# RWKV units of a decoder layer: v, the scaled key and the scaled keys turned by block-exchanging transfers and VectorE instead of TensorE

## The chip, the cores and the metric

One core of one Trainium2 chip runs one launch of the kernel. The metric is the device time of that launch in microseconds (us). The kernel before was run three times: 1602.31, 1606.76 and 1600.2 us, median 1602.31. A further execution ran under the profiler; its own time was 1607.54 us, and its trace spans 1605.8 us.

## The reference

The program is one layer of a decoder for a prompt of 1024 tokens and eight sample requests of eight tokens, at width 1024, in fp32:

```python
h = rms_norm(x, norm_mix) * (1 + sc) + sh
P = h @ w_in                      # 1792 RWKV columns, 512 pool columns, 2 x 1024 gates
o_r = rwkv7_branch(...)           # 8 heads of 64: r, decay, k, v, kk, a
o_p = pool_branch(...)
merged = sigmoid(g_r) * (o_r @ w_br_rwkv) + sigmoid(g_p) * (o_p @ w_br_pool)
x = x + gt * (merged @ w_out)
x = x + gt * (square(relu(h2 @ w_ff1)) @ w_ff2)
# in the RWKV branch, token by token:
sa = einsum("bhvk,bhk->bhv", S, -kk_t)
S = S * w_t + sa (x) (kk_t * a_t) + v_t (x) k_t
y = einsum("bhvk,bhk->bhv", S, r_t)
```

The outputs are the layer's result after a last norm and the new states. The recurrence over tokens is what the changed functions belong to.

## The kernel before

Every activation is kept with its features on the 128 partitions and its 1088 tokens (1024 and 64) in the free dimension, in tiles called `wt`, `hx`, `px` and so on. A large product is cut into output blocks of 128 features ("jobs"); each is computed in fp32 as three matmuls (weights high by input high, high by low, low by high) over three token pieces of 364, 362 and 362 columns, so TensorE sees runs of 128x362 matmuls such as `mm<-hx,whi` and `mm<-hx,wlo`. The weights of a half job arrive in `wraw` (256 KB on SyncE's queue), ScalarE rounds them to `whi`, VectorE subtracts to `wlo`.

**Phase 1** overlaps two streams on TensorE. The back stream is jobs: all of `w_in` (its inputs are the sixteen `hx` tiles of the normed x), then eight jobs of the pool half of the branch merge ("op jobs", whose inputs `hx<-d_oph`, `hx<-d_opl` are read back from DRAM into the same sixteen buffers). The fore stream is the RWKV branch, two heads at a time, f = 0 to 3: `scores` (three units: prompt chunks 0 to 7, the sample tokens, prompt chunks 8 to 15; a chunk is 64 tokens), then `main` (the inverse of each chunk's triangle, `level`, `affine`) beside `fill` (the bonus and, for f over 0, `post(f-1)`: the group norm and gate), with a sequential chain of state steps `S` per chunk running along. After the last head pair comes `post(3)`, whose two `hx` tiles (here called orr[3], high and low) are the last inputs of the RWKV half of the branch merge ("or jobs"), the first work of **phase 2**. Each or job takes its inputs in quarters, and orr[3] is the fourth quarter.

TensorE's order is written out by a planner (`Pace`) that prices every instruction with an estimate and puts fore work between job matmuls when its inputs should be ready; TensorE then executes exactly that order, and waits where an estimate was too low. The `need(...)` calls tell the planner what a fore step waits for. The other engines' orders are set by a scheduler at build time; each engine and each issuing queue executes its own order strictly.

A prompt unit (`unit`, u = 0 or 1) starts with `ra` (r and the scaled key, 128 x 8 x 2 x 64), multiplies it with `bk` (key and b) to the masked scores `ab`, `at`, `ak` (matmuls `w<-ra,bk`), scales `bk` by the chunk's end decay, and then turns three things so that tokens, not features, lie on partitions: v (16 matmuls of 64x64 with an identity, `w<-kct,wt`), the scaled key (16, `w<-kct,ra`) and the scaled `bk` (8 transposes of 128x128, `w<-kct,bk`). ScalarE copies v into `uv` and the turned `bk` into `ab`; VectorE copies the scaled key into `at`. The product `w<-uv,at` is the first reader of the turned v (scaled key and `bk` are first read in `level` and `affine`). `K.mm` is line 358, the transposes `K.tr` line 389, and every instruction of another engine is recorded at line 187.

SyncE issues nearly all transfers of this phase (`wraw`, the spills `d_x<-d`, `d_th<-px`, the reads `wt<-d_x`, `hx<-d_oph`). An fp32 matmul is recorded twice, so the counts of the profile are twice those of the program.

Of the kernel before, what the change touches and what calls it, by code (L numbers as in the profile page):

```python
# [12 lines left out]
AF = mybir.ActivationFunctionType  # L13
# [7 lines left out]
NPR = 1024  # L21
NSEQ = 8
TS = 8
NT = NPR + NSEQ * TS
# [202 lines left out]
class Room:  # L227


    wait = 0  # L230
# [91 lines left out]
class K:  # L322
# [592 lines left out]
    def unit(self, f, d, u):  # L915
# [14 lines left out]
        if prompt:  # L930
            at = Q["at"] = tl("at", [2, 64])
            ak = at[:, :, 1, :]
            strict, incl = self.kc("strict"), self.kc("incl")
        else:
            strict, incl = self.kc("strict8"), self.kc("incl8")
            ak = Q["ak"] = tl("ak", [64])
        for a in range(0, C, 4):
            m = min(4, C - a)
            us = slice(a, a + m)
            cu = slice(c0 + a, c0 + a + m)  # L940
            yield self.need(bk[:, cu], ra[:, us], banks=("w", "w"))
            pss = [self.ps("w") for _ in HB]
            for i in range(m):
                for hs, ps in zip(HB, pss):
                    self.mm(ps[:, i * 128:(i + 1) * 128], bk[hs, c0 + a + i, :, :].rearrange("p s j -> p (s j)"),
                            ra[hs, a + i, :, :].rearrange("p s j -> p (s j)"), start=True, stop=True)
            for h, (hs, ps) in enumerate(zip(HB, pss)):
                os = HB[1 - h]
                pv = ps[:, :m * 128].rearrange("p (c s j) -> p c s j", s=2, j=64)
                nc.vector.tensor_tensor(ab[:, us, h, 0:64], pv[:, :, 0, :], incl.unsqueeze(1).to_broadcast([P, m, 64]), op=ALU.mult)  # L950
                nc.vector.tensor_tensor(ak[hs, us, :], pv[hs, :, 1, :], strict[hs].unsqueeze(1).to_broadcast([64, m, 64]), op=ALU.mult)
                for b in range(2):
                    rq = slice(os.start + 32 * b, os.start + 32 * b + 32)
                    src = pv[rq, :, 1, 32 * b:32 * b + 32]
                    if prompt:
                        nc.scalar.activation(ad[rq, cu, :], src, AF.Copy)
                        if b == 0:
                            nc.scalar.activation(ao[rq, cu, :], pv[rq, :, 1, 32:64], AF.Copy)
                    else:
                        nc.vector.tensor_tensor(ad[rq, 16, :], src[:, 0, :], strict[rq, 32 * b:32 * b + 32], op=ALU.mult)  # L960
        bh = bk[:, cs, :, :].rearrange("p c s j -> p c (s j)")
        if prompt:
            nc.vector.tensor_tensor(bh, bh, end[:, cs].unsqueeze(2).to_broadcast([P, C, 128]), op=ALU.mult)
# [1 line left out]
            for s in range(2):  # L965
                nc.vector.tensor_tensor(cut8(bk[:, 16, s, :]), cut8(bk[:, 16, s, :]), end[:, 16:24].unsqueeze(2).to_broadcast([P, 8, 8]), op=ALU.mult)

        yield self.need(v[:, c0 * 64:(c0 + C) * 64], ra, banks=("w", "w"))
        ps, pa = self.ps("w"), self.ps("w") if prompt else None
        for i in range(C):  # L970
            for h, hs in enumerate(HB):
                c, os = c0 + i, HB[1 - h]
                self.mm(ps[hs, i * 64:(i + 1) * 64], v[hs, c * 64:(c + 1) * 64], ident[hs, hs], start=True, stop=True)
        if prompt:
            for i in range(C):
                for h, hs in enumerate(HB):
                    os = HB[1 - h]
                    self.mm(pa[os, i * 64:(i + 1) * 64], ra[hs, i, 1, :], ident[hs, hs], start=True, stop=True, tile_position=(hs.start, os.start))
        for h, hs in enumerate(HB):
            nc.scalar.activation(uv[hs, :, h, :], cut(ps[hs, :C * 64]), AF.Copy)  # L980
        if prompt:
            nc.vector.tensor_copy(at[:, :, 0, :], cut(pa))
        for a in range(0, C, 4):
            m = min(4, C - a)
            yield self.need(bh[:, a:a + m], wait=0, spare=900, slack=600)
            ps = self.ps("w")
            for i in range(m):
                self.tr(ps[:, i * 128:(i + 1) * 128], bh[:, a + i, :], ident)
            nc.scalar.activation(ab[:, a:a + m, :, 64:128], ps[:, :m * 128].rearrange("p (c h j) -> p c h j", h=2, j=64), AF.Copy)
        if prompt:  # L990
            yield self.need(ak, uv)
            ps = self.ps("w")
            for i in range(C):
                for h, hs in enumerate(HB):
                    os = HB[1 - h]
                    self.mm(ps[os, i * 64:(i + 1) * 64], ak[hs, i, :], uv[hs, i, h, :], start=True, stop=True, tile_position=(hs.start, os.start))
            nc.scalar.activation(at[:, :, 1, :], cut(ps), AF.Copy)

    def inverse(self, d):

# [310 lines left out]
    def heads(self):  # L1311

        for f in range(4):
# [759 lines left out]
def cut(t):  # L2073
    return t.rearrange("p (c j) -> p c j", j=64)
# [90 lines left out]
```

## Time and profile before

| | before |
|---|---|
| three runs, us | 1602.31, 1606.76, 1600.2 (median 1602.31) |
| profiled execution, own time / span | 1607.54 / 1605.8 us |
| granted TensorE clock, mean | 0.991 |
| PE busy | 1548.2 us, 96% |
| DVE busy | 1088.1 us, 68% |
| ACT busy | 664.7 us, 41% |
| POOL busy | 136.8 us, 9% |
| SyncE's DMA queue | 112448 packets, 264.65 MB, 47.4% of the 16 engines |

PE is TensorE's matmuls, PEld its weight loads (which overlap them), DVE is VectorE, ACT ScalarE, POOL GpSimd, and a q behind a name is the engine's issuing queue. Row names leave buffer numbers out: `w<-kct,bk` is a matmul into some bank `w` from tiles of the kinds `kct` and `bk`. Phase 1 ends near 747 us.

### The profile page before, as it was taken

What the parts mean: (1) busy time and instruction counts of PE and PEld (TensorE: products, weight loads), DVE (VectorE), ACT (ScalarE), POOL (GpSimd) and SP (SyncE); (2) the same over time, 40 slices, a digit from 0 to 9 for tenths busy, and PEclk for the clock granted to TensorE, in tenths of its full rate; (3) what the DMA queues carried; (4) which work ended last, traced back from release to release, by engine and by line L of the source; (5) the groups of instructions that cost most, each with busy time, mean ns of one, the idle gap of its engine ahead of it and who ended that gap; (6) DMA issues with size and microseconds to landing.
All of it is one profiled execution on the core that took longest, in us unless ns stands there. A gap on an engine that the chain in (4) does not pass through costs nothing.

```text
span 1605.8 us, 34570 instructions
## 1 busy us (share of the span) xinstructions
PE 1548.2 (96%) x14107; PEld 1459.7 (91%) x14107; DVE 1088.1 (68%) x1916; ACT 664.7 (41%) x1296; POOL 136.8 (9%) x220
## 2 busy tenths in 40 slices
PE   4999999999999999999999999999999999999997
PEld 2899888998899889889889999999999999999997
DVE  4585667866667386647542697998667796666774
ACT  4455354455235443523221573222334344334651
POOL 0110100000000000112400120000000050000000
PEclk9999999999999999999999999999999999999999
DMA  9232612343324232855885555666345996664663
GB/s 343 83 126 83 221 37 99 127 120 122 101 65 157 93 111 92 331 176 192 295 275 179 187 186 189 224 212 208 144 151 195 399 352 205 211 211 140 232 191 121
DMA packets 120031, 288.24 MB, mean 180 GB/s; under 512 B 20512, under 2 KB 24608, under 8 KB 119872
## 3 DMA queue, kind: packets, MB, share of 16 engines
q1 hardware_dynamic: 112448, 264.65, 47.4%
q10 hardware_dynamic: 5360, 14.26, 2.6%
q0 software_dynamic: 2064, 7.13, 1.3%
q8 instruction: 111, 1.82, 0.5%
q14 instruction: 48, 0.39, 0.1%
HBM read 208.70 MB, written 77.28 MB: 178 GB/s over the span
## 4 chain that ended last, share of the span: by engine, by line
PE 73%; DVE 6%; DMA 4%; issue 2%; ACT 1%; POOL 0%; SPq 0%; DVEq 0%; ACTq 0%; POOLq 0%
PE mm L358 49%; PE wc L358 13%; PE w L358 11%; DVE wt L187 2%; DMA mg<-in_w_ff 1%; DMA hx<-d_oph 1%; DMA hid<-in_w_ada_mlp 1%; DVE hv L187 1%; DVE wlo L187 1%; DMA wt<-d_x 1%; DVE bk L187 1%; DMA d_th<-px 1%; DVE hx L187 0%; POOL t L187 0%; PE w L389 0%
## 5 line engine op out<-in xcount | busy, mean ns | idle before, releaser
L358 PE MATMUL mm<-hx,whi 128*128 128x362 f32 (+2 forms) x2944 | 688.4, 321 | 5.2 <-ACT px L187 3.6
L358 PEld LDWEIGHTS mm<-hx,whi 128*128 128x128 f32 x2944 | 497.2, 190 | 28.3 <-issue 11.7
L358 PE MATMUL mm<-hx,wlo 128*128 128x362 f32 (+2 forms) x1472 | 463.2, 315 | 2.0 <-DVE wlo L187 2.0
L358 PEld LDWEIGHTS mm<-hx,wlo 128*128 128x128 f32 x1472 | 279.2, 190 | 2.6 <-DVE wlo L187 2.6
L358 PE MATMUL mm<-mg,whi 128*128 128x272 f32 (+2 forms) x1312 | 249.3, 289 | 0.0
L358 PEld LDWEIGHTS mm<-mg,whi 128*128 128x128 f32 x1312 | 205.5, 188 | 4.2 <-issue 3.4
L358 PE MATMUL mm<-mg,wlo 128*128 128x272 f32 (+2 forms) x656 | 188.5, 287 | 0.0
L358 PE MATMUL wc<-hx,whi 128*128 128x272 f32 x896 | 170.4, 287 | 0.0
L358 PEld LDWEIGHTS wc<-hx,whi 128*128 128x128 f32 x896 | 140.3, 188 | 0.0
L187 ACT ACTIVATE whi<-hid 128x512 fp32r<-128x512 f32 x128 | 80.5, 630 | 142.7 <-PE mm L358 59.8
L358 PE MATMUL wc<-hx,wlo 128*128 128x272 f32 x448 | 128.8, 287 | 1.0 <-DVE wlo L187 1.0
L358 PEld LDWEIGHTS mm<-mg,wlo 128*128 128x128 f32 x656 | 123.5, 188 | 0.0
L187 DVE TENSOR_TENSOR wlo<-hid,whi 128x512 fp32r<-128x512 f32 x128 | 88.0, 688 | 48.5 <-ACT whi L187 47.7
L187 DVE TENSOR_TENSOR wlo<-wraw,whi 128x512 fp32r<-128x512 f32 x84 | 60.6, 722 | 60.8 <-ACT whi L187 60.1
L358 PE MATMUL w<-hx,whi 128*128 128x272 f32 (+1 forms) x480 | 97.8, 298 | 0.0
L187 ACT ACTIVATE whi<-wraw 128x512 fp32r<-128x512 f32 x100 | 62.8, 628 | 78.1 <-PE mm L358 47.8
L358 PEld LDWEIGHTS wc<-hx,wlo 128*128 128x128 f32 x448 | 84.2, 188 | 1.2 <-DVE wlo L187 1.2
L187 POOL TENSOR_TENSOR hx<-hx,rs 128x64 f32<-128x64 f32 x24 | 34.8, 1452 | 568.6 <-DMA mg<-in_w_ff 361.5
L358 PEld LDWEIGHTS w<-hx,whi 128*128 128x128 f32 x480 | 77.9, 190 | 0.0
L358 PEld LDWEIGHTS mm<-mg,hx 128*128 128x128 f32 x576 | 73.0, 188 | 5.2 <-issue 5.0
L358 PE MATMUL mm<-mg,hx 128*128 128x272 f32 (+2 forms) x576 | 75.7, 290 | 0.0
L187 ACT ACTIVATE px<-mm 128x362 f32<-128x362 f32 (+3 forms) x113 | 46.2, 435 | 70.5 <-PE mm L358 66.2
(274 smaller groups left out, 2315.5 us busy)
## 6 DMA issues: line engine op xcount, KB each, us to landing
t<-d_t SPq DMA_DIRECT2D x56, 544.0 KB, 4.7
hid<-in_w_ff SPq DMA_DIRECT2D x110, 256.0 KB, 3.7
d_t<-hx SPq DMA_DIRECT2D x102, 272.0 KB, 2.2
hid<-in_w_ff SPq DMA_DIRECT2D x42, 512.0 KB, 3.6
wraw<-in_w_in SPq DMA_DIRECT2D x68, 256.0 KB, 2.8
mg<-in_w_ff SPq DMA_DIRECT2D x58, 256.0 KB, 5.4
hid<-in_w_ada_mlp SPq DMA_DIRECT2D x24, 512.0 KB, 5.2
d_th<-px SPq DMA_DIRECT2D x22, 544.0 KB, 3.0
```

What stands on the lines that cost most here:

```text
L187: return f(*a, **kw)
L358: return self.nc.tensor.matmul(out, lhsT, rhs, **kw)
```

## The change

In a prompt unit the 16 + 16 identity matmuls, the 8 transposes, the four ScalarE copies and the VectorE copy are gone. A new function `swap` issues four transfers on SyncE's queue, each 32 partitions x 8 chunks x 32 elements (32 KB in runs of 128 bytes), which put the 32x32 blocks of a 64x64 tile in each other's places; VectorE's transpose, which turns each 32x32 block in its place, does the rest. Per prompt unit:

- v: two swaps (8 transfers) from the DRAM copy `d_x` into the other head's half of `uv`, issued as the unit starts; two transposes of 64x8x64 into `uv`;
- the scaled key: two swaps (8 transfers) from `ra` into the second half of `ab`, after the first piece of scores; one transpose of 128x8x64 into `at`;
- the scaled `bk`: four swaps (16 transfers) from `bk` into `ab`; a new function `turn` transposes the two halves of `ab` in place (128x8x64 each), for u = 0 behind the sample unit and for u = 1 behind `inverse`.

That is 32 transfers and 5 transposes a unit, 256 and 40 in all. The sample unit keeps TensorE's way.

```diff
@@ scores
         yield from self.unit(f, d, 0)
         yield from self.unit(f, d, 2)
+        yield from self.turn(d["qs"][0]["bt"])
         yield from self.unit(f, d, 1)
@@ unit
             ak = at[:, :, 1, :]
+            rest = [uv[hs, :, 1 - h, :] for h, hs in enumerate(HB)]
+            for h, hs in enumerate(HB):
+                self.swap(rest[h], cut(self.d_x[8 + f][hs, c0 * 64:(c0 + C) * 64]))
...
+            if prompt and a == 0:
+                for h, hs in enumerate(HB):
+                    self.swap(ab[HB[1 - h], :, 0, 64:128], ra[hs, :, 1, :])
...
-        yield self.need(v[:, c0 * 64:(c0 + C) * 64], ra, banks=("w", "w"))
-        ps, pa = self.ps("w"), self.ps("w") if prompt else None
-        for i in range(C):
+        if prompt:
+            yield self.need(*rest, ab[:, :, 0, 64:128], banks=(), spare=2000)
             for h, hs in enumerate(HB):
-                c, os = c0 + i, HB[1 - h]
-                self.mm(ps[hs, i * 64:(i + 1) * 64], v[hs, c * 64:(c + 1) * 64], ident[hs, hs], start=True, stop=True)
+                nc.vector.transpose(uv[hs, :, h, :], rest[h])
+            nc.vector.transpose(at[:, :, 0, :], ab[:, :, 0, 64:128])
...
         if prompt:
-            for i in range(C):
-                for h, hs in enumerate(HB):
-                    os = HB[1 - h]
-                    self.mm(pa[os, i * 64:(i + 1) * 64], ra[hs, i, 1, :], ident[hs, hs], start=True, stop=True, tile_position=(hs.start, os.start))
-        for h, hs in enumerate(HB):
-            nc.scalar.activation(uv[hs, :, h, :], cut(ps[hs, :C * 64]), AF.Copy)
-        if prompt:
-            nc.vector.tensor_copy(at[:, :, 0, :], cut(pa))
-        for a in range(0, C, 4):
-            m = min(4, C - a)
-            yield self.need(bh[:, a:a + m], wait=0, spare=900, slack=600)
+            bt = [ab[:, :, h, 64:128] for h in range(2)]
+            for h, hs in enumerate(HB):
+                for g in HB:
+                    self.swap(bt[h][g], bh[hs, :, g])
...
-            for i in range(m):
-                self.tr(ps[:, i * 128:(i + 1) * 128], bh[:, a + i, :], ident)
-            nc.scalar.activation(ab[:, a:a + m, :, 64:128], ps[:, :m * 128].rearrange("p (c h j) -> p c h j", h=2, j=64), AF.Copy)
...
+    def turn(self, bt):
+        yield self.need(*bt, banks=(), wait=0, spare=2000)
+        for t in bt:
+            self.nc.vector.transpose(t, t)
+
+    def swap(self, dst, src):
+        for a in range(2):
+            for b in range(2):
+                self.nc.sync.dma_start(dst[32 * b:32 * b + 32, :, 32 * a:32 * a + 32], src[32 * a:32 * a + 32, :, 32 * b:32 * b + 32])
@@ main, in heads
                 yield from self.inverse(d)
+                yield from self.turn(d["qs"][1]["bt"])
                 yield from self.level(d)
```

The planner orders TensorE's work anew. Its estimates in place, the program's orders differ in these places.

First, TensorE in the first prompt unit (f = 0, u = 0), behind its second scores product. Before (`w_1315` is the bank of v, `w_1316` of the scaled key, `w_1358` and `w_1364` of `bk`, `hx_219` and `hx_220` are inputs of a `w_in` job):

```order
L358 MATMUL w_1315<-kct,wt_1172 64x64 x16
L358 MATMUL w_1316<-kct,ra_1046 64x64 x16
L358 MATMUL mm_1202<-hx_219,whi_1182 128x364
L358 MATMUL mm_1202<-hx_220,whi_1182 128x364
L358 MATMUL mm_1202<-hx_219,wlo_1183 128x364
L358 MATMUL mm_1203<-hx_219,whi_1182 128x362
L358 MATMUL mm_1203<-hx_220,whi_1182 128x362
L358 MATMUL mm_1203<-hx_219,wlo_1183 128x362
L389 MATMUL w_1358<-kct,bk_1015 128x128 x4
L389 MATMUL w_1364<-kct,bk_1015 128x128 x4
```

In the changed program, at the same place, the job goes on and the unit's next TensorE work is its product:

```order
L358 MATMUL mm_1364<-hx_207,whi_1279 128x362
L358 MATMUL mm_1364<-hx_208,whi_1279 128x362
L358 MATMUL mm_1364<-hx_207,wlo_1280 128x362
L358 MATMUL mm_1362<-hx_209,whi_1279 128x364
L358 MATMUL mm_1362<-hx_210,whi_1279 128x364
L358 MATMUL mm_1362<-hx_209,wlo_1280 128x364
L358 MATMUL w_1405<-uv_1178,at_1179 64x64 x16
```

Second, VectorE in the same head pair in the changed program, from the scaling of u = 0's `bk` (`bk_1015<-bk_1015,end_1014 128x1024`) to the second of its two transposes in `turn` (`ab_1177<-ab_1177`); `at_1503<-ab_1501` is the scaled key of u = 1, and the rows with `w_1444` and `w_1445` are the sample unit's masks.

```order
L187 TENSOR_TENSOR bk_1015<-bk_1015,end_1014 128x1024
L187 STREAM_TRANSPOSE at_1503<-ab_1501 128x8x64
L187 TENSOR_TENSOR wlo_1343<-wraw_1340,whi_1342 128x512
L187 SCALAR_TENSOR_TENSOR d_1352<-px_1207,part,d_1352 128x1024
L187 SCALAR_TENSOR_TENSOR ds_1353<-px_1207,part,d_1352 128x64
L187 STREAM_TRANSPOSE ab_1177<-ab_1177 128x8x64
L187 TENSOR_TENSOR ab_1426<-w_1444,kct 128x64
L187 TENSOR_TENSOR ak_1428<-w_1444,kct 64x64
L187 TENSOR_TENSOR iv_1174<-w_1444,kct 32x32 x2
```

Five more rows of masks, `bk` of the sample, one `wlo` and one transpose of `iv` follow before the second half. The copy `at<-w` that stood in this stretch is gone, and each half of `turn` waits in VectorE's order for its eight transfers.

Third, TensorE at the end of phase 1. Before, behind the last but one group-norm sums (`w<-wt,sw`; `hx_7487`, `hx_7489` are inputs of an op job, `S` the state steps, `w<-wt,kct` the sums of `post(3)`):

```order
L358 MATMUL w_8190<-wt_8129,sw_8127 128x362
L358 MATMUL mm_8152<-hx_7487,whi_7968 128x362
L358 MATMUL mm_8152<-hx_7489,whi_7968 128x362
L358 MATMUL mm_8152<-hx_7487,wlo_7969 128x362
L358 MATMUL wc_8081<-S_8181,ra_6924 64x64 x2
L358 MATMUL wc_8082<-ra_6924,S_8181 64x64 x2
L358 MATMUL w_8202<-wt_8129,sw_8127 128x362
L358 MATMUL w_8206<-wt_7127,kct 128x364
```

Now, from the same place:

```order
L358 MATMUL w_8256<-wt_8210,sw_8208 128x362
L358 MATMUL wc_8162<-S_8247,ra_7009 64x64 x2
L358 MATMUL wc_8163<-ra_7009,S_8247 64x64 x2
L358 MATMUL w_8269<-wt_8210,sw_8208 128x362
L358 MATMUL w_8273<-wt_7232,kct 128x364
L358 MATMUL wc_8162<-S_8263,ra_7009 64x64 x2
L358 MATMUL wc_8163<-ra_7009,S_8263 64x64 x2
L358 MATMUL w_8283<-wt_8272,kct 128x364
L358 MATMUL wc_8162<-S_8277,ra_7009 64x64 x2
L358 MATMUL wc_8163<-ra_7009,S_8277 64x64 x2
L358 MATMUL wc_8162<-S_8292,ra_7009 64x64 x2
L358 MATMUL wc_8163<-ra_7009,S_8292 64x64 x2
```

Behind these stand four sums `w<-wt,kct 128x362` and then the or jobs without a break. Before, 405 job matmuls stood from here to the end of the or jobs, 123 of them belonging to op jobs; now it is 282, the or jobs' own. The 123 have gone ahead of this place.

More of the change, by code (lines that the diff above doesn't have):

```diff
@@ L986, in unit @@
             ps = self.ps("w")
[L987 to L989 removed]
+            self.tr(ps[:, 0:128], bh[:, 0, :], ident)
+            nc.scalar.activation(ab[:, 0, :, 64:128], ps[:, 0:128].rearrange("p (h j) -> p h j", h=2), AF.Copy)
         if prompt:
```

10 lines of the change are left out of this document (added).

## The prediction

> **What bounds the kernel now.** The page's busy shares come first, then its chain of work that ended last:
>
> ```profile
> PE 1548.2 (96%) x14107; PEld 1459.7 (91%) x14107; DVE 1088.1 (68%) x1916; ACT 664.7 (41%) x1296; POOL 136.8 (9%) x220
> PE 73%; DVE 6%; DMA 4%; issue 2%; ACT 1%; POOL 0%; SPq 0%; DVEq 0%; ACTq 0%; POOLq 0%
> ```
>
> TensorE is busy for 96% of the span and carries 73% of the chain, so TensorE time that is really taken away should show. But a share over the span doesn't say that it stays so where the work is taken out. The table of busy time by stretch gives the two stretches that matter, the middle of phase 1 and its last 47 us:
>
> ```profile
> 100.00:600.00 500.00, 482.55 (x5373) 435.58 (x5374) 342.69 (x628) 229.03 (x491) 31.10 (x91) 0.99 0.33 112
> 700.00:747.00 47.00, 47.00 (x400) 41.38 (x399) 30.37 (x56) 13.36 (x26) 7.14 (x9) 1.00 0.44 155
> ```
>
> The columns are length, then PE, PEld, DVE, ACT and POOL. TensorE is nearly full in both, VectorE has 31% free in the first. The planner has just enough job matmuls to cover the RWKV branch to its last instruction. That is the point on which the forecast turns.
>
> **What the change removes.** On TensorE, the timeline of the first unit shows what the blocks cost the job stream around them, from start to start:
>
> ```profile
> 134.77 0.32 PE L358 MATMUL mm<-hx,wlo 128*128 128x362 f32 x1
> 135.03 0.97 PE L358 MATMUL w<-kct,wt 64*64 64x64 f32 x26
> ...
> 135.96 0.98 PE L358 MATMUL w<-kct,ra 64*64 64x64 f32 x27
> 136.87 0.60 PE L358 MATMUL mm<-hx,whi 128*128 128x364 f32 x2
> ...
> 137.79 0.33 PE L358 MATMUL mm<-hx,wlo 128*128 128x362 f32 x1
> 137.96 1.03 PE L389 MATMUL w<-kct,bk 128*128 128x128 f32 x8
> 138.75 0.58 PE L358 MATMUL mm<-hx,whi 128*128 128x362 f32 x2
> 139.17 0.32 PE L358 MATMUL mm<-hx,wlo 128*128 128x362 f32 x1
> 139.33 0.49 PE L358 MATMUL mm<-hx,whi 128*128 128x364 f32 x2
> ```
>
> From 139.17 to 139.33 one job matmul takes 0.16 to 0.17 us. From 134.77 to 136.87 are 2.10 us, so v and key delay the jobs by 1.93; from 137.79 to 138.75 are 0.96, so the transposes delay them by 0.79. That is 2.7 us a unit and would be 21.8 for eight; where a block shares its place with a state step it saves less, where the transposes stand in two halves or wait a little, more. I take **21.5 us**. The summed busy time of the three groups is an upper end, since fp32 matmuls overlap in the records:
>
> ```profile
> L358 PE MATMUL w<-kct,wt x272: 218/218/267, 135.0 to 625.6; 64*64 64x64 f32 x136
> L358 PE MATMUL w<-kct,ra x256: 218/218/267, 135.8 to 626.4; 64*64 64x64 f32 x128
> L389 PE MATMUL w<-kct,bk x68: 270/272/329, 138.0 to 628.9; 128*128 128x128 f32 x68
> ```
>
> All of it lies ahead of 629 us. On ScalarE go 32 copies, 19 us, off the path at 41% busy: no term. On VectorE the copy goes and five transposes come:
>
> ```profile
> L187 DVE COPY at<-w x8: 690/692/692, 137.0 to 627.8; 128x512 f32<-128x512 f32 x8
> L187 DVE STREAM_TRANSPOSE iv<-iv 128x512 f32<-128x512 f32 x16 | 16.2, 1051 | 0.0
> L187 ACT ACTIVATE uv<-w 64x512 f32<-64x512 f32 x16 | 9.5, 592 | 11.4 <-PE w L358 11.4
> ```
>
> The row of `iv` has the same 512 elements a partition, so five transposes take 5.3 us at most, less 0.7: +4.6 us a unit, +37 in all, 7% of the 500 us, inside the 31% that is free. Busy time alone costs nothing; waits at the transposes do.
>
> **What the transfers cost.** Nothing here moves 128-byte runs between partitions. The nearest rows are a load of 60 KB in 1024 runs of 60 bytes and a store of 32 KB in long runs:
>
> ```profile
> L187 SPq DMA_DIRECT2D psm<-in_spool x4: 378/381/429, 24.6 to 421.5; - x4
> DMA to landing us min/median/max: 2.3/2.7/7.6
> ...
> DMA to landing us min/median/max: 2.4/2.5/7.0
> d_x<-ds SPq DMA_DIRECT2D x14, 32.0 KB, 2.5
> ```
>
> (The second landing row is that of `ds`.) Small runs cost little: 1024 of them land in 2.3 us when the queue is free. I take 0.38 us to issue and 2.5 us to land; 7.0 us, the worst 32 KB row, is the other end. By this, 8 transfers have landed 8 x 0.38 + 2.5 = 5.5 us after the first may go, 16 after 8.6 us.
>
> A rule of the Trainium skill ("DMA: Bandwidth & Descriptors", Rules for kernel authors) speaks against the change: transpose with the hardware's DMA transpose, not with a plain transfer in a rearranged pattern, which is put at a factor of 19. By that rule a 32 KB swap that moves in some 0.1 us (an estimate from 403 GB/s in the rows of 656 us below) would need near 2 us of all engines, 16 swaps over 30 us, and the second rival below would be certain. The landing of the 1024 short runs does not bear that out; the runs here are twice as long, and VectorE does the element-wise part.
>
> SyncE issues 32 transfers a unit, 12.2 us of its time. It has cover, since most of phase 1 it waits for a free weight buffer, as the table of waits up to 700 us shows:
>
> ```profile
> SPq L187 <- DVE wlo L187: 255.1, 51, 18.9
> PE wc L358 <- DVE S L187: 5.9, 6, 1.9
> ```
>
> (The second row is TensorE's longest wait between 100 and 700 us.) If a late `wraw` broke that cover, TensorE would stop for what is missing; I put it at nothing, for 255 us of waiting stand against 98 us of issues.
>
> **The added waits.** v and key are asked for early, behind some 40 job matmuls: nothing. The wait that counts is `turn` for u = 0. In VectorE's new order only a key transpose, a `wlo`, a `d` and a `ds` stand between the scaling of `bk` and the first half of `turn`:
>
> ```profile
> 126.01 1.27 DVE L187 SCALAR_TENSOR_TENSOR d<-px,part,d 128x1024 f32<-128x1024 f32 x1
> 129.88 0.69 DVE L187 TENSOR_TENSOR wlo<-wraw,whi 128x512 fp32r<-128x512 f32 x1 [1.62 <-ACT whi L187]
> ```
>
> With 1.05 + 0.69 + 1.27 + 0.28 = 3.3 us of cover VectorE stands still for 5.5 - 3.3 = 2.2 us; the sample's masks and the next `wlo` queue behind it, and TensorE waits for those. The second half has 8.9 us of cover against 8.6: nothing. TensorE has up to a half job (36 matmuls, 5.9 us) in hand for `wlo`, but none for state steps. I charge 1 us of the 2.2 for each of four such units: **4 us**, between 0 and the second rival. For u = 1 `turn` stands behind the inverse, long after: nothing, except at f = 3, where the swaps queue behind eleven 544 KB loads of `hx`.
>
> **The end of phase 1.** In the old trace the last group-norm sums start at 714.87, the last VectorE step of orr[3] ends at 746.71:
>
> ```profile
> 714.87 1.49 PE L358 MATMUL w<-wt,sw 128*128 128x364 f32 x4
> 736.06 0.77 PE L358 MATMUL w<-wt,kct 128*128 128x362 f32 x2
> ...
> 712.80 0.28 DVE L187 SCALAR_TENSOR_TENSOR S<-S,end,wc 128x64 f32<-128x64 f32 x1 [1.95 <-PE wc L358]
> 714.87 0.28 DVE L187 SCALAR_TENSOR_TENSOR S<-S,end,wc 128x64 f32<-128x64 f32 x1 [1.79 <-PE wc L358]
> 737.99 2.42 DVE L187 RECIPROCAL wt<-wt 128x182 f32<-128x182 f32 x2
> 746.17 0.54 DVE L187 TENSOR_TENSOR hx<-wt,hx 128x362 fp32r<-128x362 f32 x1 [0.57 <-ACT hx L187]
> ```
>
> Behind the sum at 736.06 stand 39 + 27 job matmuls (10.9 us) before the first that reads orr[3], at 747.6: TensorE never waits. The change moves 123 job matmuls (20.3 us) ahead of the 714.87 place and takes 21.5 us out, so this place comes at 714.9 + 20.3 - 21.5 = 713.7: **hardly earlier**. Then only state steps and `post(3)` are left, and TensorE stands mostly idle. Two adjacent state steps are 2.07 us apart (712.80 to 714.87): four of them to 8.3 us, the first mean sum at 8.7. Two pieces then follow each other: mean, square, sum, root (0.5 us each with its way) to 11.6; two RECIPROCAL pairs of 2.42 and a product each on VectorE to 17; the rest of the last piece, 746.71 - 740.41 = 6.3 us before, of which some 1.5 were the op jobs' additions, to about 22. I take 22.5: orr[3] at 736.2, where it was needed at 747.6. The gain is **11.4 us**, not 21.5.
>
> What an idle TensorE costs after is in the table by stretches of 2 us at 656, where it stood 2 us:
>
> ```profile
> 656.00:658.00 2.00, 0.47 (x56) 0.35 (x43) 2.00 (x3) 0.00 (x0) 0.00 (x0) 1.00 1.01 403
> 658.00:660.00 2.00, 1.54 (x12) 1.50 (x13) 1.51 (x2) 0.20 (x1) 0.00 (x0) 0.71 1.03 413
> 660.00:662.00 2.00, 2.00 (x9) 2.00 (x8) 0.00 (x0) 1.86 (x4) 0.83 (x1) 0.50 1.02 407
> 662.00:664.00 2.00, 2.00 (x13) 2.00 (x13) 0.15 (x1) 1.81 (x2) 0.44 (x1) 0.93 1.01 389
> ```
>
> The granted clock (the last but two column) then lacks 0.29, 0.50 and 0.07 of 2 us each: **1.7 us**. Sum: -11.4 + 1.7 + 4 = -5.7 us. Against the profiled execution's 1607.5 that is 1601.8; the median of the runs stands 5.2 below that execution, so the forecast is **1597 us**.
>
> **The rivals.** *All of it stays.* If `post(3)` alone takes 12 us from the last sums, not 22.5, orr[3] never holds TensorE and 21.5 come off: 1581. For it speaks that VectorE loses the op jobs' additions there; against it that four state steps and two RECIPROCAL pairs are 13 us alone. Chance 0.22.
>
> *The transfers land late, and it is slower.* At 7.0 us the eight land 10.0 us after `bk`, VectorE stands 6.7 at the first half of each u = 0 `turn`; if TensorE idles 5 of these and takes the 1.7 for the clock behind it, four times 6.7 = 27, and -11.4 + 1.7 + 27 = +17: 1620. It decides from an idle of 2.4 us per `turn`, that is from a landing near 5 us. Large loads on the same queue speak for it (7.0 and 7.6 were seen), against it the medians of 2.5 and 2.7. At f = 3 the swaps behind the `hx` loads could add up to 5. Chance 0.24.
>
> *It only moves idle.* If the end takes as long bare as before (31.8 us from 714.87), since VectorE and ScalarE set it and not the jobs between, 1.2 - 1.7 is left, with a little of the waits: 1603. VectorE's 30.4 busy of 47 us speak for it, though part of that were the jobs' additions. Chance 0.12.
>
> **How the numbers follow.** The forecast has 0.42, and 1590 to 1602 as its own range; 0.17 of it lies under 1594.3. About 0.5%, 8 us, is what a measurement of this kernel can tell from no change. Faster: 0.22 + 0.17 = 0.39; same: 0.25 + 0.12 = 0.37; slower: 0.24. From 1579 to 1614 are the forecast, the third case, most of the first (0.18) and the near part of the second (0.08): 0.80.
>
> **What would show it.** In the new profile: no `w<-kct,ra`, and `w<-kct,wt` only for the sample; landing of `ab<-bk` near 2.5 us (right) or above 5 (second rival); waits of VectorE for a DMA at `ab<-ab` near 2 us, four times; the last group-norm sums near 714; TensorE's busy time in the 22 us behind that under a half, then a clock of 0.5 for some 4 us. I would be wrong altogether if TensorE waited somewhere in the middle for weights, which I priced at nothing.

## The result and the profile after

The changed kernel takes 1651.48 us (median of 1650.85, 1651.48 and 1659.63) against 1602.31: a ratio of 1.0312, interval 1.0292 to 1.0331. It is slower by 3%; the forecast was 1597 us. The profiled execution took 1651.48 us, its span is 1649.6.

Busy time, the chain by engine, and SyncE's queue (packets, MB, share of the 16 engines) on the page of the changed kernel:

```profile
PE 1545.9 (94%) x13531; PEld 1448.8 (88%) x13531; DVE 1109.7 (67%) x1948; ACT 647.5 (39%) x1264; POOL 136.2 (8%) x220
PE 68%; DVE 14%; DMA 9%; issue 3%; SPq 3%; ACT 3%; POOL 0%; DVEq 0%; ACTq 0%; POOLq 0%
q1 hardware_dynamic: 182080, 273.05, 49.6%
```

The identity products are gone (576 fewer records on PE: two for each of 256 products, one for each of 64 transposes), yet PE's busy time falls by 2.3 us only, and the part of the span in which PE is not busy grows from 1605.8 - 1548.2 = 57.6 to 1649.6 - 1545.9 = 103.7 us. So the change shows as 46 us of new idle, and as a gain of some 20 us of matmuls that a lower clock eats: it fell from 0.991 to 0.976, and 1.5% of 1548 is 23 us. Attributed from each matmul's start to the next start, the blocks that went held 20.6 us, idle rose by 47 and everything else by some 18.

Where the idle lies is seen in the table by stretches of the changed kernel (length, PE, PEld, DVE, ACT, POOL busy, clock, DMA share, GB/s):

```profile
100.00:600.00 500.00, 460.19 (x4703) 413.05 (x4702) 328.20 (x599) 204.01 (x436) 28.91 (x88) 0.96 0.41 121
350.00:450.00 100.00, 76.30 (x950) 65.26 (x949) 60.15 (x93) 42.55 (x80) 4.04 (x12) 0.86 0.27 84
434.00:438.00 4.00, 0.08 (x1) 0.00 (x0) 4.00 (x8) 0.20 (x2) 0.00 (x0) 0.77 0.22 25
438.00:442.00 4.00, 0.00 (x0) 0.00 (x0) 3.96 (x8) 0.73 (x2) 0.04 (x1) 0.50 0.00 0
442.00:446.00 4.00, 0.00 (x0) 0.00 (x0) 3.99 (x9) 0.73 (x2) 0.97 (x2) 0.50 0.00 0
446.00:450.00 4.00, 2.73 (x5) 1.68 (x6) 2.73 (x5) 1.49 (x2) 0.00 (x0) 0.50 0.00 0
450.00:454.00 4.00, 4.00 (x42) 2.23 (x42) 4.00 (x8) 1.85 (x4) 0.00 (x0) 0.60 0.46 140
770.00:792.00 22.00, 14.71 (x82) 10.45 (x80) 14.80 (x24) 8.30 (x16) 1.56 (x2) 0.84 0.11 39
```

The kernel before had, in the middle one of these stretches:

```profile
350.00:450.00 100.00, 95.29 (x1002) 83.88 (x1000) 61.10 (x105) 42.18 (x90) 3.89 (x11) 0.98 0.33 110
```

From 100 to 600 us PE was busy for 482.55 us, now 460.19. From 350 to 450 it is idle for a quarter of the time, where it was idle for a twentieth, and from 434 on it stands still while VectorE is full. The clock falls with it and is at 0.60 still in the stretch after work has begun again. Who is waited for, in TensorE's waits up to 820 us (total, times, longest), of the changed kernel:

```profile
PE w L358 <- ACT wt L187: 21.0, 11, 9.1
PE w L358 <- DVE sq L187: 19.2, 1, 19.2
PE w L358 <- issue: 14.2, 2, 13.2
PE w L358 <- DVE px L187: 8.0, 3, 5.5
PE wc L358 <- DVE S L187: 7.4, 7, 2.2
```

and of the kernel before:

```profile
PE w L358 <- DVE sq L187: 19.8, 1, 19.8
PE wc L358 <- DVE S L187: 5.9, 6, 1.9
...
PE w L358 <- DVE px L187: 3.0, 3, 1.8
...
PE w L358 <- issue: 2.9, 2, 2.0
```

The wait for `sq` is the kernel's start and the same in both. The new waits are for `wt` and `px`: tiles of the head pairs' preparation, of the group norm and of the pool, not the turned tiles. The turned tiles do hold up VectorE, as the groups of its transposes show (busy, mean ns, then the idle ahead of them and its releasers):

```profile
L187 DVE STREAM_TRANSPOSE ab<-ab 128x512 f32<-128x512 f32 x16 | 11.3, 706 | 13.7 <-DMA ab<-bk 13.4 <-issue 0.3
L187 DVE STREAM_TRANSPOSE uv<-uv 64x512 f32<-64x512 f32 x16 | 11.2, 701 | 7.5 <-DMA uv<-d_x 7.3
L187 DVE STREAM_TRANSPOSE at<-ab 128x512 f32<-128x512 f32 x8 | 5.7, 710 | 9.8 <-DMA ab<-ra 8.3 <-DMA uv<-d_x 1.3 <-issue 0.2
```

That is 30 us of standing still for transfers, at all three kinds of tile. Their issue (min/median/max ns) and landing are in the view of the tile `ab`:

```profile
L187 SPq DMA_DIRECT2D ab<-bk x128: 585/609/1712, 135.9 to 687.6; - x128
L187 SPq DMA_DIRECT2D ab<-ra x64: 585/608/1644, 110.0 to 657.3; - x64
...
DMA to landing us min/median/max: 1.9/1.9/10.0
```

One transfer of a swap between two places of the core's own memory takes SyncE 0.61 us to issue and lands 1.9 us later (the median of both kinds; the longest took 10.0). SyncE's timeline at f = 1 (start, duration) shows what stands in line:

```profile
318.96 1.90 SPq L187 DMA_DIRECT2D ab<-bk  x3
320.96 0.53 SPq L187 DMA_DIRECT2D d_th<-px  x1
321.54 9.71 SPq L187 DMA_DIRECT2D ab<-bk  x13
...
332.70 0.43 SPq L187 DMA_DIRECT2D wt<-d_y  x1
333.18 0.87 SPq L187 DMA_DIRECT2D wraw<-in_w_in  x1
```

The sixteen issues of one unit hold the queue for 12 us, and two stores, a read back and the next weights come out between or behind them. At f = 3 this stops TensorE. On the timelines of SyncE, ScalarE and TensorE:

```profile
672.58 15.62 SPq L187 DMA_DIRECT2D ab<-bk  x16
...
690.27 0.47 SPq L187 DMA_DIRECT2D wt<-d_y  x1
```

```profile
697.54 1.30 ACT L187 ACTIVATE wt<-wt 128x364 fp32r<-128x364 f32 x3 [5.90 <-DMA wt<-d_y]
```

```profile
698.10 1.85 PE L358 MATMUL w<-wt,bones 128*128 128x364 f32 x4 [9.09 <-ACT wt L187]
```

The read back `wt<-d_y` brings the input of a group norm. SyncE issues it 2 us after the last swap; ScalarE, which rounds it, and TensorE, which sums it, wait for it. The 9.09 us are the longest wait for `wt` in the table above. The wait of 13.2 us, which is longer still, has another cause, shown further below.

### The profile page after: what moved, and what is told of

Its sections match the earlier page's. It is cut to its first block, busy times and chain, and to the rows that moved or that the text cites. A ratio compares the mean times of both kernels' runs of the same rounds, so it can differ in the third digit from the quotient of the medians.

```text
span 1649.6 us, 33794 instructions
## 1 busy us (share of the span) xinstructions
PE 1545.9 (94%) x13531; PEld 1448.8 (88%) x13531; DVE 1109.7 (67%) x1948; ACT 647.5 (39%) x1264; POOL 136.2 (8%) x220
## 3 DMA queue, kind: packets, MB, share of 16 engines
q1 hardware_dynamic: 182080, 273.05, 49.6%
## 4 chain that ended last, share of the span: by engine, by line
PE 68%; DVE 14%; DMA 9%; issue 3%; SPq 3%; ACT 3%; POOL 0%; DVEq 0%; ACTq 0%; POOLq 0%
PE mm L358 46%; PE w L358 11%; PE wc L358 10%; DVE wt L187 4%; DVE hx L187 3%; SPq L187 3%; DMA hid<-in_w_ff 2%; DMA d_t<-hx 1%; DVE wlo L187 1%; ACT wt L187 1%; DVE bk L187 1%; DMA wt<-d_x 1%; DVE hv L187 1%; DMA hid<-in_w_ada_mlp 1%; DMA wt<-d_y 1%
```

## The experiments

Two theories stood against each other. **Waits**: the swaps come late or hold SyncE and VectorE, so TensorE idles. **Order**: the planner, told of other instructions, wrote TensorE's order anew, and the new order costs whatever stands in place of the blocks. In all tables "free" is the span less PE's busy time, of the profiled execution: 57.6 before, 103.7 after. A caution holds for all runs: what is left out also lets the scheduler order VectorE and SyncE a little differently, so effects do not add up exactly.

### The change with less of one cost, and one order without the change

One transfer in place of the four of each swap, in the changed TensorE order (the planner is still told of four; the 32x32 blocks don't change places):

```diff
         for a in range(2):
             for b in range(2):
-                self.nc.sync.dma_start(dst[32 * b:32 * b + 32, :, 32 * a:32 * a + 32], src[32 * a:32 * a + 32, :, 32 * b:32 * b + 32])
+                if self.clocks.on:
+                    self.clocks.op("sync", "dma_start", (dst[32 * b:32 * b + 32, :, 32 * a:32 * a + 32], src[32 * a:32 * a + 32, :, 32 * b:32 * b + 32]), {})
+        self.tc.nc.sync.dma_start(dst, src)
```

> Each swap is one plain transfer of 64x8x64 (128 KB) instead of four of 32x8x32; the exchange of the 32x32 blocks is left out. 64 transfers in place of 256, TensorE's order is that of the change, the 40 transposes stay. Theory A (SyncE: a swap transfer takes 0.61 us to issue, 32 of them 19 us a unit, and every load behind them in the queue comes late): most of the 49 us come back, 1600 to 1625. Theory B (VectorE: 22 us of added transposes and the order they stand in): little, since they are all there, at or above 1640. Theory C (the new order on TensorE and VectorE, whatever the transfers cost): at or above 1640 as well.

The swaps on GpSimd's queue instead of SyncE's:

```diff
-                self.nc.sync.dma_start(dst[32 * b:32 * b + 32, :, 32 * a:32 * a + 32], src[32 * a:32 * a + 32, :, 32 * b:32 * b + 32])
+                self.nc.gpsimd.dma_start(dst[32 * b:32 * b + 32, :, 32 * a:32 * a + 32], src[32 * a:32 * a + 32, :, 32 * b:32 * b + 32])
```

> The 256 swap transfers go out on GpSimd's queue instead of SyncE's; everything else and TensorE's order are as in the change. Theory A (SyncE's queue): 1600 to 1630 if GpSimd issues them as quickly; if GpSimd takes over 1 us for each, VectorE's waits for swaps grow and it is no faster than the change, while SyncE's own loads are on time again. Theories B and C: 1640 to 1660.

The sixteen transposes in place planned, but not issued:

```diff
         for t in bt:
-            self.nc.vector.transpose(t, t)
+            if self.clocks.on:
+                self.clocks.op("vector", "transpose", (t, t), {})
```

> The 16 in-place transposes of the scaled bk are left out (so is their result); the 128 transfers that feed them still go out, and TensorE's order is that of the change. VectorE loses 11.3 us of work and 13.4 us of waiting for transfers. Theory B: TensorE's idle time falls by 15 us or more, 1620 to 1635. Theory A: the transfers still crowd SyncE, 1640 to 1652. Theory C: 1640 to 1652.

And the kernel before, with nothing changed but the lead that the planner gives to the turning of v and key, so that its order is written anew:

```diff
-        yield self.need(v[:, c0 * 64:(c0 + C) * 64], ra, banks=("w", "w"))
+        yield self.need(v[:, c0 * 64:(c0 + C) * 64], ra, banks=("w", "w"), spare=2000)
```

> The kernel before, with one number of the planner changed: the step that turns v and the scaled key is planned 2000 ns after its inputs are ready instead of 300. No work is added or taken out, only the order moves. Theory C (any new order costs, since the old one fits the measured times): 1615 or more. Theories A and B: within 8 us of the kernel before.

| run | us | before beside it | free |
|---|---|---|---|
| one transfer a swap | 1663.83 | 1604.15 | 112.9 |
| GpSimd's queue | 1658.95 | 1604.15 | 112.1 |
| no transposes in place | 1667.87 | 1604.15 | 111.6 |
| before, other lead | 1620.16 | 1604.15 | 64.7 |

Each is one run. A quarter of the issues, another queue, or no transposes: none of the three comes back towards 1604, and none lies below the three runs of the change (1650.85 to 1659.63). On GpSimd's queue VectorE's waits for swaps are 1.5 us, not 30, and yet nothing is won. TensorE's waits of that kernel:

```profile
PE wc L358 <- DVE S L187: 16.1, 6, 8.4
PE w L358 <- issue: 14.7, 2, 13.2
PE mm L358 <- DVE px L187: 13.8, 1, 13.8
PE w L358 <- DVE px L187: 13.1, 3, 7.8
```

The wait of 13.2 us is there again, as in the other two. The 9.09 us at f = 3 do go with the transfers: without the transposes the same stop is 8.32 us, while with a quarter of the issues and on GpSimd's queue no wait for `wt` is over 4.0. But other waits grow instead: on GpSimd's queue one at `S` is 8.4 us and one at `px` 13.8. And a mere rewriting of the order of the kernel before cost 16 us. The waits theory alone falls.

### The two halves apart

First, swaps and transposes as in the change, but the planner is told of the old products, so that TensorE's order is that of before with the blocks struck out (the sample unit's step moves slightly):

```diff
-            yield self.need(*rest, ab[:, :, 0, 64:128], banks=(), spare=2000)
+            yield self.need(v[:, c0 * 64:(c0 + C) * 64], ra, banks=("w", "w"))
+            ps, pa = self.ghost("w"), self.ghost("w")
...
-            nc.vector.transpose(at[:, :, 0, :], ab[:, :, 0, 64:128])
+            real.transpose(at[:, :, 0, :], ab[:, :, 0, 64:128])
```

> All 256 transfers and 40 transposes of the change, and no identity products, but the planner is told of the old identity products, copies and transposes (which aren't issued) and not of the transfers, so TensorE's order is that of the kernel before with the eight blocks struck out. Theory C (the order): most of the loss goes, 1580 to 1612. Theories A and B (the transfers on SyncE, the transposes on VectorE): their cost is all here, so 1630 or more.

Second, the reverse: the planner is told of the swaps, TensorE does the old products at the places where the change has its steps:

```diff
+                self.clocks.op("vector", "transpose", (at[:, :, 0, :], ab[:, :, 0, 64:128]), {})
...
+                    rn.tensor.matmul(ps[hs, i * 64:(i + 1) * 64], v[hs, c * 64:(c + 1) * 64], ident[hs, hs], start=True, stop=True)
...
-            nc.vector.transpose(at[:, :, 0, :], ab[:, :, 0, 64:128])
+            rn.vector.tensor_copy(at[:, :, 0, :], cut(pa))
```

> The reverse: no transfers and no transposes; v, scaled key and scaled bk are turned by TensorE as in the kernel before, but the planner is told of the change's transfers and transposes, so TensorE's order is the change's with the eight blocks put in where VectorE's transposes stood. Theory C: as slow as the change or slower by the blocks' 21 us where TensorE is full there, 1640 to 1675. Theories A and B: near the kernel before, 1600 to 1620.

Third, the change with the pool's columns asked for later, as a cure for the wait at `px`:

```diff
-                yield self.need(z[:, c0:c0 + m], plw, zs, wait=0, spare=6000)
+                yield self.need(z[:, c0:c0 + m], plw, zs, wait=0, spare=22000)
```

> The change, with one number of the planner moved: the pool branch's products are planned 22 us after their inputs are expected instead of 6 us, so that job matmuls stand ahead of them. Theory C in the form that the pool products wait in TensorE's order for a VectorE that is then busy with the next head pair's front: the waits at these products (13.2, 5.5 and some of 1 us) go, 1625 to 1640. If other places of the new order take over what is freed: 1645 to 1655. Theories A and B: 1640 to 1655, since neither transfers nor transposes change.

| run | us | before beside it | ratio | free |
|---|---|---|---|---|
| swaps, old order | 1631.89 | 1607.61 | 1.016 (1.014 to 1.018) | 87.8 |
| products, new order | 1660.22 | 1607.61 | one run | 96.2 |
| pool later | 1672.31 | 1607.61 | one run | 106.0 |

Both halves cost by themselves. The new order is as slow with the old products in it, without any transfer, as with the swaps; the swaps in the old order cost 1.6%. The cure was none: the wait of 13.2 us is gone (none at `px` is over 3.5), but others took its place, and the time is above every range that was expected of it. How the swaps cost in the old order, at f = 2, is on SyncE's timeline of that run:

```profile
441.98 10.39 SPq L1071 DMA_DIRECT2D ab<-bk  x16
...
454.76 5.79 SPq L1071 DMA_DIRECT2D ab<-ra  x8
```

and on VectorE's, with the idle in front of the instruction in brackets:

```profile
462.26 0.71 DVE L1007 STREAM_TRANSPOSE at<-ab 128x512 f32<-128x512 f32 x1 [4.25 <-DMA ab<-ra]
462.99 0.42 DVE L187 TENSOR_TENSOR ab<-w,kct 128x256 f32<-128x256 f32 x1
```

The key's swaps of u = 1 are issued behind the `bk` swaps of u = 0 and two stores. The last is issued at 460.5, the transpose waits, and the masks of the unit's scores queue behind it, and with them the rest of the branch. With two more such stops, of 3.81 and 2.26 us in front of the transposes in place, VectorE stands still for 10.3 us between 444 and 462. TensorE still runs then. From 462 to 512 VectorE is busy for 44.28 of 50 us, so it makes up little, and at 512.19 TensorE has waited 9.84 us for its `hv`. That the second stop comes from the first is argued from this, not tested by itself.

### Transfers and transposes apart, in the old order

TensorE's order as in the first of these three, but neither transfer nor transpose is issued; GpSimd fills the turned tiles with zeros. Then the same with the 40 transposes alone, and with the 256 transfers alone.

```diff
+            z = self.tc.nc.gpsimd
+            z.memset(at[:, :, 0, :], 0.0)
...
-                self.nc.sync.dma_start(dst[32 * b:32 * b + 32, :, 32 * a:32 * a + 32], src[32 * a:32 * a + 32, :, 32 * b:32 * b + 32])
+                pass
```

> TensorE's order of e5 (the order of before with the eight blocks of identity products struck out), but without transfers and without transposes: v, scaled key and scaled bk aren't turned, GpSimd fills their places with zeros. What striking the blocks is worth if the replacement were free. If TensorE's time bounds phase 1 as the prediction had it: 1580 to 1588 (20.6 us less). If the freed time mostly turns into waits for the recurrence's own chain: 1592 to 1606.

> As e8, with the 40 transposes on VectorE, on places that GpSimd has filled with zeros, and no transfers. Theory B (VectorE's added work and order): most of the way from e8 to e5, 1615 to 1635. Theory A (the transfers): within 8 us of e8.

> As e8, with the 256 transfers on SyncE and no transposes (TensorE's products wait for the transfers themselves). Theory A (SyncE's 0.61 us for each issue and what waits behind them): most of the way from e8 to e5, 1615 to 1635. Theory B: within 8 us of e8. If neither e9 nor e10 is over 10 us above e8, it is the two together: transposes that wait in VectorE's order for transfers.

| run | us | before beside it | ratio | PE busy | free |
|---|---|---|---|---|---|
| nothing in place | 1597.41 | 1607.11 | 0.9944 (0.9928 to 0.9961) | 1528.1 | 67.6 |
| transposes | 1597.93 | 1607.11 | 0.9956 (0.9937 to 0.9974) | 1532.0 | 68.4 |
| transfers | 1606.11 | 1607.11 | 0.9993 (0.9978 to 1.0009) | 1537.3 | 67.2 |

This is the ceiling of the idea in this order: even when what replaces the blocks is free, it wins 0.6%. PE's busy time falls by 20.1 us, as the blocks' price says, and half of that, 10.0, comes back as idle. The waits for the state step `S`, the longest of this kernel after its start, say where:

```profile
PE wc L373 <- DVE S L187: 15.3, 7, 9.6
```

The 9.6 us begin at 549.7. TensorE's and VectorE's timelines of this kernel end it so:

```profile
559.26 0.48 PE L373 MATMUL wc<-S,ra 64*64 64x64 f32 x4 [9.57 <-DVE S L187]
```

```profile
557.66 1.35 DVE L187 SCALAR_TENSOR_TENSOR wt<-wt,part,wt 128x1088 f32<-128x1088 f32 x1
558.93 0.27 DVE L187 SCALAR_TENSOR_TENSOR S<-S,end,wc 128x64 f32<-128x64 f32 x1
```

The state step, 0.27 us long, stands in VectorE's order behind the preparation of the next head pair, whose 128x1088 step is the row ahead of it. VectorE's timeline has no gap between 549 and 559. TensorE reaches the place earlier without the blocks, and VectorE doesn't. The transposes add 0.5 us, nothing. The transfers alone add 8.7. Transfers and transposes together, 1.016 against 0.9944, add some 34: 25 of them are neither's own. That they are VectorE standing in its order in front of transposes, for transfers that SyncE issues one behind the other, is what the next run tests.

### A quarter of the issues, nothing in the new order, another plan, other prices

If the serial issue is what VectorE waits for, then one transfer a swap in the old order (64 instead of 256) must bring much of it back; the edit is that of the first run, on the kernel with swaps in the old order.

> As e5 (order of before without the blocks, all 40 transposes), but each swap is one plain transfer of 64x8x64 instead of four of 32x8x32, so 64 issues in place of 256; the exchange of the 32x32 blocks is left out. If the 25 us that e5 lies above what e9 and e10 add up to are VectorE standing in its order for transfers that SyncE takes 0.61 us each to issue: VectorE's waits for transfers fall from 33 us to under 15, and the time to 1598 to 1612. If they come from the transposes and transfers meeting in some other way, not from the number of issues: 1622 or more.

The new order with nothing in place of the blocks, planned as in the change (GpSimd fills the places with zeros, and the transposes are left out in the same way as the transfers):

```diff
...
-                self.nc.sync.dma_start(dst[32 * b:32 * b + 32, :, 32 * a:32 * a + 32], src[32 * a:32 * a + 32, :, 32 * b:32 * b + 32])
+                if self.clocks.on:
+                    self.clocks.op("sync", "dma_start", (dst[32 * b:32 * b + 32, :, 32 * a:32 * a + 32], src[32 * a:32 * a + 32, :, 32 * b:32 * b + 32]), {})
```

> TensorE's order of the change, but nothing stands in for the blocks: no products, no transfers, no transposes (GpSimd fills the places with zeros; v, scaled key and scaled bk aren't turned). The counterpart of e8 (1597) in the new order. If the new order itself costs: 1625 to 1645. If it costs only because transfers and transposes are late for it: 1575 to 1600, faster than e8, as the end of phase 1 was forecast.

The kernel before, with the default lead of every step at nothing:

```diff
-    def need(self, *aps, banks=("w",), wait=1000, spare=300, slack=0):
+    def need(self, *aps, banks=("w",), wait=1000, spare=0, slack=0):
```

> The kernel before with another number of the planner changed: every step of the RWKV branch and the pools that is planned 300 ns after its inputs is planned with 0. No work is added or taken out. If the order of before is one that fits the measured times and most others do not: 1612 or more, as e4 (1620). If e4 was slow because it moved the branch later: within 6 us of before.

And the change with the planner told what the swaps and transposes were measured to take:

```diff
-            t += 2000 + out.shape[0] * n * 4 / 220 if out.shape[0] <= P else 4000
+            if out.shape[0] == 32:
+                t = self.place("sync", t, 610) + 610
+                t += 1900
+            else:
+                t += 2000 + out.shape[0] * n * 4 / 220 if out.shape[0] <= P else 4000
...
-                ns = 2.05 * n
+                ns = (1.4 if out.tensor.name.startswith(('ab', 'at', 'uv')) else 2.05) * n
```

> The change, with the planner's prices of the swaps set to what the trace shows: 0.61 us to issue one behind the other and 1.9 us to land (it had 2.15 us for all at once), 0.70 us for such a transpose (it had 1.05). Same transfers and transposes, another order. If the new order costs since it is built on these wrong prices: 1605 to 1630. If it costs since it puts the branch further behind the jobs, or since the other prices don't hold in any new order: 1640 to 1670.

| run | us | before beside it | ratio | free |
|---|---|---|---|---|
| old order, one transfer a swap | 1612.18 | 1608.35 | 1.0025 (1.0008 to 1.0041) | 75.6 |
| new order, nothing in place | 1636.68 | 1608.35 | 1.019 (1.016 to 1.022) | 95.0 |
| before, default lead 0 | 1628.53 | 1608.35 | 1.0137 (1.0111 to 1.0162) | 70.4 |
| change, measured prices | 1663.2 | 1608.35 | 1.0359 (1.0327 to 1.039) | 111.6 |

A quarter of the issues brings some 20 of the 34 us back in the old order, where the same edit in the new order brought nothing. VectorE's waits for swaps fall from 33 to 20 us there, where under 15 was expected, and 13 us of the price stay. So the number of issues is most of it, and the way from there to the time is only in part these waits. The new order costs 1.9% with nothing in it, some 39 us more than the old order with nothing in it. Better prices for the swaps do not mend it, and a second rewriting of the order of before costs 20 us. No version tried beats the kernel before with its work complete.

**Why the new order costs** can be read at one place, the 13.2 us. In the kernel before, VectorE's timeline there is

```profile
410.85 1.34 DVE L187 SCALAR_TENSOR_TENSOR wt<-wt,part,wt 128x1088 f32<-128x1088 f32 x1
...
417.05 1.32 DVE L187 TENSOR_TENSOR d<-px 128x1038 f32<-128x1038 f32 x1
...
423.91 0.17 DVE L187 COPY px<-zf 128x7 f32<-128x7 f32 x1
```

The pool's chain from `d<-px` to the last copy into `px` runs as one block of 7.0 us, behind the 128x1088 step that follows the last piece of the next head pair's `bk`. With the new order and nothing in place of the blocks:

```profile
415.18 1.24 DVE L187 TENSOR_TENSOR d<-px 128x1038 f32<-128x1038 f32 x1
...
416.59 1.96 DVE L187 RECIPROCAL wt<-wt 128x182 f32<-128x182 f32 x2
...
439.27 0.17 DVE L187 COPY px<-zf 128x7 f32<-128x7 f32 x1
439.35 1.34 DVE L187 SCALAR_TENSOR_TENSOR wt<-wt,part,wt 128x1088 f32<-128x1088 f32 x1
```

The same chain takes 24 us, since the head pair's preparation now lies between its links: the 128x1088 step stands behind it. TensorE's order has the pool's product next, and on TensorE's timeline of this kernel that shows as

```profile
439.54 2.76 PE L358 MATMUL w<-px,plw 128*128 128x364 f32 x4 [13.22 <-issue]
```

TensorE starts 0.1 us after the copy's end. (The profile says "issue" since it has no releaser for it; the operand `px` and the copy's end name it.) The changed kernel has the same: its chain runs from 422.92 to 447.17, 24 us, and on TensorE's timeline

```profile
447.27 2.76 PE L358 MATMUL w<-px,plw 128*128 128x364 f32 x4 [13.19 <-issue]
```

What put the one chain into the other can be read from the order, though no run tests it by itself. The pool's products `w<-px,plw` begin behind 1086, 1293, 1536 and 1752 job matmuls (`mm<-hx`) before, and behind 1086, 1320, 1533 and 1752 in the change: they keep their place among the jobs, to within 27. The branch doesn't. The first `w<-ab,at` of the four head pairs stands behind 732, 1317, 1962 and 2481 job matmuls before, and behind 795, 1413, 2076 and 2607 in the change: 63 to 126 later, or 10 to 21 us at 0.165 us each. So the pool's chain meets the preparation of the next head pair on VectorE, and its last link stands behind that. The 9.6 us above, in the old order, are of the same kind: a short step that TensorE needs, behind the preparation of a head pair. It isn't the jobs' lead alone that costs: in the kernel before with default lead 0 the first `w<-ab,at` stand behind 723, 1317, 1893 and 2418, at the old place or up to 69 job matmuls earlier, and that order costs 20 us too, with stops of 6.6 us at `px` and 5.8 at `S`.

## Why the prediction was wrong, point by point

- **What the removal is worth on TensorE: right.** Predicted 21.5 us; 20.6 measured from start to start, and 20.1 of busy time in the kernel with nothing in place of the blocks.
- **"TensorE is nearly full, so its time should show": half wrong.** The prediction itself named the share over a long stretch as weak evidence, but looked for the hole only behind the last sums. Of 20.1 us removed 10.0 became idle even with the order kept, and one stop of 9.6 us in the middle of the phase is new.
- **The middle of the phase, 4 us: the step that failed.** It priced only the waits of `turn` and took the moved order as free. The new order alone costs some 39 us over the struck old order, the swaps in the old order some 34. Together the last group-norm sums came at 769.4 instead of the predicted 713.7, 56 us late. That is all of the distance between the forecast of 1597 and the measured 1651 us; the stretch behind that place was right to 1 us.
- **SyncE's issue at 0.38 us: mis-sized.** The row was a load from DRAM. Between two places of the core's memory it is 0.61 us, so 16 transfers have landed after 11.7 us (16 x 0.61 + 1.9), not 8.6.
- **SyncE's 255 us of waiting as cover: right for the weights, wrong as a rule.** TensorE's waits for `wlo` went from 1.8 to 3.7 us, near the nothing that was put down for them. But the cover is a sum over the phase, and what counts is when each issue comes out of the queue: `bk` of one unit stood ahead of the key of the next, and at f = 3 ahead of the read back for which TensorE stopped 9.09 us. The prediction named the swaps at f = 3 as an exception, for another reason (the loads of `hx`), and gave them no price in its sum.
- **One wait of 2.2 us at four `turn`s: mis-sized.** There were 30 us of VectorE waits: 13.4 at `turn`, in 7 waits of up to 4.0, and the rest at v and key, which were put at nothing.
- **The transfer itself, 2.5 us to land: about right** (1.9 us in the median between two places of the core's memory, 2.2 from DRAM). The share of SyncE's queue rose from 47.4% of 1605.8 to 49.6% of 1649.6 us, 57 us for 256 transfers or 0.22 each, by estimate: two to three times the time by bytes. By the rule of the Trainium skill ("DMA: Bandwidth & Descriptors", Rules for kernel authors) the prediction's estimate was near 2 us of all engines for each. This trace doesn't agree with the factor of 19 for this exchange, in which runs of 128 bytes stay whole.
- **VectorE's transposes inside its free share: right,** 0.5 us when alone, which is within the noise. They take 0.70 us each, not 1.05.
- **The end of phase 1: right in mechanism and size.** The last sums and the last step of orr[3] in the changed kernel, on TensorE's and on VectorE's timeline:

```profile
769.39 1.49 PE L358 MATMUL w<-wt,sw 128*128 128x364 f32 x4
```

```profile
792.31 0.54 DVE L187 TENSOR_TENSOR hx<-wt,hx 128x362 fp32r<-128x362 f32 x1 [0.57 <-ACT hx L187]
```

- From 769.39 to 792.85 are 23.5 us; 22.5 had been predicted. Two of its signs missed. PE's busy share was to be under a half there; it was 14.71 of 22 us. The low clock was to come behind it; it came inside (0.84 over these 22 us, 1.00 over the next 4).
- **The rivals.** "The transfers land late" had the right sign, but its mechanism did not occur: it decides from a landing near 5 us, and the medians stay at 1.9 and 2.2. By these rows the wait at `turn` came from the issue instead. That a rewritten order costs by itself was no rival at all, though the order's difference had been laid out. What could have raised it is the job count: 123 job matmuls had moved ahead of the branch, and they were used for the end of the phase only.

**What stays open.** Why this planner's other orders cost, of those tried, is shown at one place, 13 of some 39 us, and by its pattern, not traced to one of its rules; where that wait was taken away alone, others came. Ten kernels here have the new order or another than that of before, and all are slower by about 1% or more; measured prices for the swaps did not help. Six of the ten share the TensorE order of the change, so few orders were tried. The parts do not add: new order 39 and swaps 34 make 73 over the struck kernel, where the change has some 59 (1.0312 against 0.9944).

## What to carry to other kernels

Where an order is written out ahead and executed strictly, a local edit is two changes, the work and the order: first build the old order with the block struck out and nothing in its place, which here would have shown a ceiling of 0.6% before any replacement was written, then the new order with nothing in it. Count how far each stream moves against the other at several places, not at the end alone, since a chain that becomes ready inside another engine's block is paid for in full. Price transfers by a row with the same kind of end points, and by the queue's order: so many issues times the issue time before the one that is waited for.

## What the runs showed of the hardware

- A transfer of 32 x 8 x 128 bytes inside the core's memory takes SyncE 0.61 us to issue (585 ns at least); one plain transfer of 64 x 8 x 64 elements in its place 0.61 to 0.63. The same transfer read from DRAM takes 0.45 in the median.
- VectorE's transpose of 128x8x64 takes 0.71 us, that of `iv`, with as many elements, 1.04 in the same kernel.
- TensorE's granted clock was 0.77 in the 4 us in which it stopped, 0.50 for the next 12 and 0.60 for the 4 behind. From 447.27, where it starts again, that is 2.73 us at half and 4 at 0.60: a stop of 13 us costs some 3 us more after it has ended.
- The 256 transfers without the transposes left TensorE's free time as it was (67.2 against 67.6 us), with no wait of TensorE for a swap in its table; its busy time grew by 9.2 us. In the two profiles the clock is 0.985 against 0.991, but over the ten runs of each the medians are 0.990 and 0.9905 while the times differ by 8.7 us. So a price in clock isn't shown, and why the matmuls take longer is open.
